# Two-layer hybrid decoder: value halves added after a trip through memory, query zeros kept, softmax reciprocals as a power on GpSimd

## The chip, the cores and the metric

The kernel runs on one core of a Trainium2 chip, as one launch for both layers. The metric is the device time of that launch in microseconds. The engines are named as the profile names them: PE (TensorE), PEld (its weight loads), DVE (VectorE), ACT (ScalarE), POOL (GpSimd), SP (SyncE, which issues the DMAs).

## What is computed

Two decoder layers over 1024 tokens of width 1024, all in fp32 accuracy. A layer projects x into four groups of heads with a token mixer each: gMLP (a), latent attention with a rotary part (b), dilated sliding-window attention (c) and a chunkwise mLSTM (d). The four results are concatenated, projected, added to the residual and normalised, and a SwiGLU feed-forward follows. Only b, c and the projection are touched here.

```python
def reference(x, positions, w_in, ...):
    for l in range(DEPTH):
        z = x @ w_in[l]
        z_a, z_b, z_c, z_d = jnp.split(z, [A_COLS, A_COLS + B_COLS, A_COLS + B_COLS + C_COLS], axis=-1)
        y_a = _gmlp_mixer(z_a, a_ln_g[l], a_ln_b[l], a_ws[l], a_bs[l])
        y_b = _mla_mixer(z_b, positions, b_q_norm[l], b_kv_norm[l], b_w_uq[l], b_w_ukv[l])
        y_c = _dilated_mixer(z_c, positions)
        y_d = _mlstm_mixer(z_d, d_conv_w[l], d_conv_b[l], d_igate_b[l], d_fgate_b[l])
        y = jnp.concatenate([y_a, y_b, y_c, y_d], axis=-1) @ w_out[l]
        x = _layer_norm(DEEPNORM_ALPHA * x + y, ln1_g[l], ln1_b[l])
        h = (jax.nn.silu(x @ w_gate[l]) * (x @ w_up[l])) @ w_down[l]
        x = _layer_norm(DEEPNORM_ALPHA * x + h, ln2_g[l], ln2_b[l])
    return x
```

## The kernel before, in words

PE multiplies fp32 numbers as a high and a low part (type fp32r), so most operands exist twice: ACT casts the high part, and DVE or POOL subtracts it from the source to get the low one (`split`, L145; for weights `prep_w`, L131 and L136). A tile framework puts the instructions of ACT, DVE, POOL and SP into an order; the order of PE in the attention is the one in which the code issues them (`manual_schedule` with `MAN`). Each engine runs its instructions strictly in order.

**Attention (`attn`).** A layer has four groups of two heads: G0 and G1 for the dilated mixer (mask `maskC`), G2 and G3 for the latent one (`maskB`, and a rotary part `R`, `QR`). A group is 16 rows, a row being one head with 128 queries; the 64 rows of a layer are numbered through, 0 to 63. Row by row `scores` multiplies queries and keys (tile `sc`), DVE adds the mask and takes the row minimum `mn` (L815), ACT takes the exponential and its sum `rs` (L819), DVE the reciprocal of the sum (L821), POOL multiplies the row `P` by it (L822). Three rows later `turn` transposes `P` on PE (`pt`, L839) and ACT and DVE split it into `PH` and `PL`; two rows later `values` multiplies with the values for each pair of rows (`pv`, L860). The value matrix holds its high part in columns 0 to 63 and its low part in 64 to 127, so `pv` comes out as two halves of 64 partitions that have to be added: ACT copies both into one tile `tmp` (L872, L873), POOL adds them (L874). For G0 and G1 a DMA writes the sum to `ys` in memory (L876), for G2 and G3 it stays in the tiles `Yb`. Four of the 32 pairs are `full`: their values are plain fp32 and only one half exists.

**Queries.** `put_q` fills two tiles for each head (q1, q2). q1 holds the high part of 64 rows twice, in both halves of the partitions (L786 and L788, ACT, from PSUM), q2 the low part in one half (L787) and zeros in the other (L789, POOL, a multiplication of the identity by 0). `qk_tiles` takes new tiles for each group.

**Jobs between rows.** Work for later groups is cut into jobs that `fill` spreads over the rows of the current one: in G0 the end of the projection `zc` and the queries and keys of G1; in G1, from `b_vqr_jobs`, the rotary queries of the latent groups (`rot`: PE `prb`, then rotation on DVE, L1026 to L1032, into `qr`), their values (`vals`: PE `pvb`) and the transposition of `qr` (`turn`: PE `ptr`, L1043, evacuated by L1046 and L1047). Both layers have the same program.

**Projection (`out_proj`).** The first four weight tiles `wO` are split during the last rows of the attention (L131 on ACT, L136 on POOL). `ysplit` loads the mixers' results from `ys` into tiles `yr` (pool "r", two buffers, shared with the raw weights) and splits them into `yT` (L145); g counts the quarter of the columns, and only g of 1 comes from `Yb`.

```python
        jobs = [start]
        for t2 in range(4):
            jobs += [f(rot, t2), f(vals, t2), f(turn, t2)]
        jobs += [f(rotk, half) for half in range(2)]
```

Of the kernel before, what the change touches and what calls it, by code (L numbers as in the profile page):

```python
# [13 lines left out]
L = 2  # L14
# [43 lines left out]
class Net:  # L58
# [89 lines left out]
    def consts(self):  # L148
        nc, cp, io = self.nc, self.cp, self.io
        self.ident = cp.tile([128, 128], F32, name="ident")  # L150
        nc.sync.dma_start(self.ident, io["c_ident"])
        self.identr = cp.tile([128, 128], F32R, name="identr")
        nc.vector.tensor_copy(self.identr, self.ident)
        sel = cp.tile([128, 8], F32, name="self32")
        nc.sync.dma_start(sel, io["c_sel"])
        self.sel = cp.tile([128, 8], F32R, name="sel")
        nc.vector.tensor_copy(self.sel, sel)
        self.mhalf = cp.tile([128, 8], F32, name="mhalf")
        nc.vector.memset(self.mhalf, -0.5)
        self.triu = cp.tile([128, 128], F32, name="triu")  # L160
# [621 lines left out]
    def put_q(self, pq, q1, q2, cols):  # L782
        nc = self.nc
        for hh in range(2):
# [3 lines left out]
            nc.scalar.copy(q1[hh][o, cols], pq[r, :])  # L788
            nc.gpsimd.tensor_scalar(out=q2[hh][o, cols], in0=self.ident[o, 0:1].to_broadcast([64, 512]), scalar1=0.0, scalar2=None, op0=ALU.mult)  # L789

    def attn(self, groups):
# [6 lines left out]
        def scores(n):  # L798
# [21 lines left out]
            def norm():  # L820
                nc.vector.reciprocal(rs[:, 1:2], rs[:, 0:1])  # L821
# [27 lines left out]
        def values(n):  # L849
# [25 lines left out]
            if spill is not None:  # L875
                nc.sync.dma_start(spill, y)  # L876
# [100 lines left out]
    def b_vqr_jobs(self, ct, w, out):  # L977
# [98 lines left out]
    def attention(self, l, zc, zjobs, ct):  # L1076
        nc, io = self.nc, self.io
        yv = lambda Y, g: [Y[0][:, g, :], Y[1][:, g, :]]
        bb = {}
        G = [dict(scale=sc, ahead=a, pp=p, full=f) for sc, a, p, f in zip((0.125, 0.125, 96 ** -0.5, 96 ** -0.5), AHEADS, PPS, FULL)]  # L1080
        for f in self.prep_c_jobs(zc[0], G[0]):
# [6 lines left out]
        def start0():  # L1088
            m = self.u("maskC")
            nc.sync.dma_start(m, io["c_maskC"])  # L1090
            G[0].update(mask=m, spill=(l, 0))
            self.jobs = zjobs + self.prep_c_jobs(zc[1], G[1])

        def start1():
            G[1].update(mask=G[0]["mask"], spill=(l, 1))
            w = box["w"] = self.b_weights(l)

            def st():
                bb["qk"] = self.qk_tiles("E", ("E", "B"))
            self.jobs = self.b_vqr_jobs(ct, w, bb) + [st] + self.b_qk_jobs(0, ct, w, bb, "qk")  # L1100

        def start2():
            m = self.u("maskB")
            nc.sync.dma_start(m, io["c_maskB"])
            box["Yb"] = [self.u("Yb", F32, "A").rearrange("p (a n) -> p a n", a=2) for _ in range(2)]
            bb["qk1"] = self.qk_tiles("A")
            G[2].update(mask=m, Y=yv(box["Yb"], 0), qk=bb["qk"], V=bb["V"][0], R=bb["R"], QR=bb["QR"][0])
            self.jobs = self.b_qk_jobs(1, ct, box["w"], bb, "qk1")

        def start3():  # L1110
            G[3].update(mask=G[2]["mask"], Y=yv(box["Yb"], 1), qk=bb["qk1"], V=bb["V"][1], R=bb["R"], QR=bb["QR"][1])
# [61 lines left out]
    def out_proj(self, l, Yb, xsrc):  # L1173
# [432 lines left out]
    def build(self):  # L1606
        self.open(B=8, w=10, r=2, E=10)
        T = [[None, None] for _ in range(KD)]
        for l in range(self.layers):
# [9 lines left out]
            self.dump(f"yb{l}", yb)  # L1619
# [5 lines left out]
def layouts(inp):  # L1625
# [42 lines left out]
    o["c_ident"] = np.eye(128, dtype=np.float32)  # L1668
    sel = np.zeros((128, 8), np.float32)
# [40 lines left out]
```

## Time and profile before

| what | value |
|---|---|
| median of 3 runs | 2476.17 us (2475.47 to 2478.26) |
| the profiled execution: time, span | 2477.19 us, 2475.5 us |
| PE busy | 2373.0 us (96%) |
| DVE, ACT, POOL busy | 67%, 42%, 53% |
| mean granted clock of PE | 0.983 |
| attention, layer 1 | about 260 to 460 us of the span |
| attention, layer 2 | about 1495 to 1695 us of the span |

Shares of the whole span say little here: most of the span is feed-forward, in which PE is busy without a gap. What the change can win or lose is read in the two stretches of attention and just behind them, where PE has gaps. The profile names for each gap the instruction whose end released it; "P L822" is the multiplication of a row by its reciprocal, "mn L815" its minimum, and so on.

### The profile page before, as it was taken

The page shows a single profiled execution, that of the slowest core. Times are in us where ns is not written, and L with a number is a line of the kernel's source. Part 1 is how long each engine was busy: PE and PEld are TensorE (multiplying, and loading weights), DVE is VectorE, ACT ScalarE, POOL GpSimd, SP SyncE. Part 2 cuts the span into 40 slices and gives each one's busy share as a digit, 9 for nine tenths or more (in the row PEclk, how much of TensorE's full clock was granted, in tenths as well). Part 3 has the DMA queues.
Part 4 walks back from the last instruction along what each step waited for, and adds up shares of the span by engine and source line. Part 5 has one row for each costly group of instructions (what it writes and reads, how often), then busy time and mean ns, then how long its engine had stood idle before and what let it go on. Part 6 is the DMA issues. An engine that isn't in the chain of part 4 may idle for free.

```text
span 2475.5 us, 33577 instructions
## 1 busy us (share of the span) xinstructions
PE 2373.0 (96%) x11820; PEld 1992.1 (80%) x11820; DVE 1662.9 (67%) x2978; ACT 1040.0 (42%) x2102; POOL 1308.8 (53%) x1172
## 2 busy tenths in 40 slices
PE   9999878998999999999999999789989999999997
PEld 9889867786888888788797898677868888887886
DVE  7743687478665664789957436873786655647999
ACT  6322669534323323543333226685343333235432
POOL 2124536667554554786622245366675554547865
PEclk9999999998999999999999999999989999999999
DMA  4111001421332322743221110014213323327431
GB/s 165 53 34 48 18 10 56 162 94 43 128 111 81 111 98 97 268 164 128 95 69 53 39 50 11 18 56 154 102 44 119 111 81 114 107 101 257 166 120 68
DMA packets 82198, 235.27 MB, mean 95 GB/s; under 512 B 10784, under 2 KB 13152, under 8 KB 82032
## 3 DMA queue, kind: packets, MB, share of 16 engines
q1 hardware_dynamic: 82032, 233.14, 27.3%
q8 instruction: 94, 1.54, 0.3%
q14 instruction: 72, 0.59, 0.1%
HBM read 172.78 MB, written 60.33 MB: 94 GB/s over the span
## 4 chain that ended last, share of the span: by engine, by line
PE 76%; DVE 11%; ACT 5%; POOL 4%; issue 3%; DMA 1%; POOLq 0%; DVEq 0%; ACTq 0%; SPq 0%
PE gu L123 33%; PE dn L123 13%; PE zc L123 5%; PE po L123 4%; PE zvo L568 4%; PE zdq L520 3%; PE za L123 3%; PE zb L123 2%; PE sc L123 2%; PE pv L860 2%; DVE P L815 1%; PE pt L839 1%; ACT P L819 1%; DVE PL L145 1%; POOL x L1132 1%
## 5 line engine op out<-in xcount | busy, mean ns | idle before, releaser
L123 PE MATMUL gu<-T,fc 128*128 128x512 f32 x2640 | 639.6, 399 | 17.0 <-POOL T L1340 5.9
L123 PEld LDWEIGHTS gu<-T,fc 128*128 128x128 f32 x2640 | 502.4, 191 | 140.6 <-POOL T L1340 8.8
L1265 POOL TENSOR_TENSOR fc<-fw,fc 128x512 fp32r<-128x512 f32 x264 | 374.2, 1421 | 362.4 <-ACT fc L1264 358.1
L123 PE MATMUL dn<-dc,dc 128*128 128x512 f32 x1512 | 354.8, 397 | 4.9 <-DVE dc L1265 4.9
L123 PEld LDWEIGHTS dn<-dc,dc 128*128 128x128 f32 x1512 | 286.2, 189 | 73.1 <-DVE dc L1265 5.7
L1264 ACT CAST fc<-fw 128x512 fp32r<-128x512 f32 x264 | 162.8, 621 | 409.2 <-PE gu L123 264.1
L123 PE MATMUL gu<-B,fc 128*128 128x512 f32 x1056 | 260.6, 395 | 0.0
L145 POOL TENSOR_TENSOR dc<-hr,dc 128x512 fp32r<-128x512 f32 x126 | 195.0, 1562 | 87.6 <-ACT dc L142 80.8
L123 PEld LDWEIGHTS gu<-B,fc 128*128 128x128 f32 x1056 | 197.8, 188 | 47.0
L1389 DVE TENSOR_TENSOR Ra<-Ra,gu 128x512 f32<-128x512 f32 x172 | 117.8, 686 | 162.7 <-PE gu L123 157.6
L822 POOL TENSOR_SCALAR P<-P,rs 128x256 f32<-128x256 f32 (+7 forms) x128 | 98.7, 775 | 125.7 <-DVE rs L821 100.3
L123 PE MATMUL po<-wh,yT 128*128 128x512 f32 x512 | 162.2, 396 | 0.0
L123 PE MATMUL zc<-wh,xT 128*128 128x384 f32 x512 | 134.0, 339 | 0.0
L136 POOL TENSOR_TENSOR wl<-raw,wh 128x768 fp32r<-128x768 f32 (+2 forms) x40 | 81.8, 2050 | 82.4 <-ACT wh L131 81.7
L123 PE MATMUL sc<-kst,q 128*128 128x512 f32 (+3 forms) x384 | 111.5, 387 | 12.5 <-DVE mn L815 12.5
L839 PE MATMUL pt<-ident,P 128*128 128x128 f32 x576 | 93.1, 287 | 23.5 <-DVE PL L145 15.0
L123 PEld LDWEIGHTS po<-wh,yT 128*128 128x128 f32 x512 | 95.7, 188 | 21.8
L1265 DVE TENSOR_TENSOR dc<-dr,dc 128x512 fp32r<-128x512 f32 x72 | 90.2, 1264 | 32.9 <-ACT dc L1264 32.8
L142 ACT CAST dc<-hr 128x512 fp32r<-128x512 f32 x126 | 77.7, 622 | 82.1 <-DMA hr<-hs 53.8
L819 ACT ACTIVATE P<-P,mn 128x256 f32<-128x256 f32 (+7 forms) x128 | 99.4, 778 | 29.1 <-DVE mn L815 28.3
L145 DVE TENSOR_TENSOR PL<-pt,PH 128x512 fp32r<-128x512 f32 (+3 forms) x176 | 95.1, 557 | 21.4 <-ACT PH L142 20.3
L123 PE MATMUL po<-wl,yT 128*128 128x512 f32 x256 | 100.2, 394 | 0.0
(377 smaller groups left out, 4999.9 us busy)
## 6 DMA issues: line engine op xcount, KB each, us to landing
fw<-in_wGU SPq DMA_DIRECT2D x88, 512.0 KB, 4.4
hr<-hs SPq DMA_DIRECT2D x142, 256.0 KB, 3.0
dr<-in_wD SPq DMA_DIRECT2D x44, 512.0 KB, 6.2
hs<-Ra SPq DMA_DIRECT2D x40, 512.0 KB, 2.9
hs<-Rb SPq DMA_DIRECT2D x22, 512.0 KB, 5.4
raw<-in_wO SPq DMA_DIRECT2D x16, 512.0 KB, 3.5
x<-x SPq DMA_DIRECT2D x16, 512.0 KB, 2.6
raw<-in_wC SPq DMA_DIRECT2D x16, 384.0 KB, 3.0
```

The source lines that it names most:

```text
L123: self.nc.tensor.matmul(out, lhsT=a, rhs=b, start=first and j == 0, stop=last and j == n - 1)
L136: (eng or nc.gpsimd).tensor_sub(lo[:, :n], raw[:, :n], f32(hi[:, :n]))
L142: nc.scalar.copy(hi, src)
L145: (lo_eng or nc.vector).tensor_sub(lo, src, f32(hi))
L520: step(lambda: nc.tensor.matmul(pz, lhsT=a, rhs=b_, start=n == 0, stop=n == 23))
L568: nc.tensor.matmul(box["p"], lhsT=a, rhs=b_, start=j == 0, stop=j == 23)
L819: nc.scalar.activation(P[:, 0:nk], P[:, 0:nk], AF.Exp, scale=-1.0, bias=m, accum_out=rs[:, 0:1])
L822: nc.gpsimd.tensor_scalar(out=P[:, 0:nk], in0=P[:, 0:nk], scalar1=rs[:, 1:2], scalar2=1.0, op0=ALU.mult, op1=ALU.mult)
L839: nc.tensor.transpose(pt[:, b * 128:(b + 1) * 128], P[:, (b0 + b) * 128:(b0 + b + 1) * 128], self.ident)
L1264: nc.scalar.copy(dst[:, 0:512], src)
L1265: lo_eng.tensor_sub(dst[:, 512:1024], src, f32(dst[:, 0:512]))
L1389: tt = lambda o, a, b, op: v.tensor_tensor(out=o, in0=a, in1=b, op=op)
```

## The change

1. **Reciprocal.** `rs` to the power of -1 on POOL (new line L828, with a tile `minus` of -1) in place of DVE's reciprocal L821. The multiplication behind it is now L829.
2. **Queries.** The second copy of the high part is a POOL copy from the first copy in SBUF (L796) in place of ACT's cast from PSUM. The zero halves are written once a tile, at its full width of 1024 columns (L780, the mask times 0), and the tiles q2 of G0 and G1 are used again by G2 and G3. `maskC` is loaded earlier.
3. **Values.** For G0, G1 and G2 ACT copies both halves of `pv` at once (128 partitions), and two DMAs write them apart to a new array `yp` (for full pairs the second DMA writes zeros). For G3 ACT copies one half and DVE adds the other half from PSUM into the one tile `Yb`.
4. **Projection.** `ysplit` loads pairs of halves from `yp` (three loads for each h, in place of one) and DVE adds them.
5. **Jobs.** `turn` of a pair of blocks comes one `rot` later; one pair of `QR` tiles moves to other pools.

Per layer that takes from DVE 64 reciprocals and gives it 8 additions of 64x256 (G3) and 6 of 128x512 (`yp`); takes from ACT 16 casts of 64x512 and turns 56 copies of 64x256 into 20 of 128x256 and 8 of 64x256; takes from POOL 16 multiplications of 64x512 and 28 additions of 64x256 and gives it 64 powers of 128x1, 16 copies of 64x512 and 4 multiplications of 64x1024. SP issues 48 writes of halves where it issued 16 of sums, and 10 loads for `ysplit` where it issued 6.

```diff
@@ qk_tiles, put_q
+    def qk_tiles(self, pool, q2=None):
+        f = lambda n: self.u(n, F32R, pool)
+        kst, q1 = [f("kst") for _ in range(2)], [f("q1") for _ in range(2)]
+        if q2 is None:
+            q2 = [f("q2") for _ in range(2)]
+            for hh in range(2):
+                o = slice(64 - 64 * hh, 128 - 64 * hh)
+                self.nc.gpsimd.tensor_scalar(out=q2[hh][o, :], in0=self.mask[o, :], scalar1=0.0, scalar2=None, op0=ALU.mult)
+        return kst, q1, q2
...
-            nc.scalar.copy(q1[hh][o, cols], pq[r, :])
-            nc.gpsimd.tensor_scalar(out=q2[hh][o, cols], in0=self.ident[o, 0:1].to_broadcast([64, 512]), scalar1=0.0, scalar2=None, op0=ALU.mult)
+            nc.gpsimd.tensor_copy(q1[hh][o, cols], f32(q1[hh][r, cols]))
@@ scores
-                nc.vector.reciprocal(rs[:, 1:2], rs[:, 0:1])
+                nc.gpsimd.tensor_tensor(out=rs[:, 1:2], in0=rs[:, 0:1], in1=self.minus, op=ALU.pow)
@@ values
+            tmp = self.t2("tmp", 256)
             if "Y" in G:
+                y = G["Y"][64 * hh:64 * hh + 64, jp * 256:(jp + 1) * 256]
+                if full:
+                    nc.scalar.copy(y, pv[0:64, 0:256])
+                else:
+                    nc.scalar.copy(tmp[0:64, :], pv[0:64, 0:256])
+                    nc.vector.tensor_tensor(out=y, in0=tmp[0:64, :], in1=pv[64:128, 0:256], op=ALU.add)
+                return
+            nc.scalar.copy(tmp[0:m, :], pv[0:m, 0:256])
+            for part in range(2):
+                dst = G["spill"][part][64 * hh:64 * hh + 64, jp * 256:(jp + 1) * 256]
+                nc.sync.dma_start(dst, self.io["c_zero"][:, 0:256] if full and part else tmp[64 * part:64 * part + 64, :])
...
-                nc.scalar.copy(tmp[0:64, 0:256], pv[0:64, 0:256])
-                nc.scalar.copy(tmp[0:64, 256:512], pv[64:128, 0:256])
-                nc.gpsimd.tensor_tensor(out=y, in0=tmp[0:64, 0:256], in1=tmp[0:64, 256:512], op=ALU.add)
@@ b_vqr_jobs
-        for t2 in range(4):
-            jobs += [f(rot, t2), f(vals, t2), f(turn, t2)]
-        jobs += [f(rotk, half) for half in range(2)]
+        jobs += [f(rot, 0), f(vals, 0)]
+        for t2 in range(1, 4):
+            jobs += [f(rot, t2), f(turn, t2 - 1), f(vals, t2)]
+        jobs += [f(rotk, 0), f(turn, 3), f(rotk, 1)]
@@ out_proj, ysplit
-                if g != 1:
+                if g in (0, 3):
...
+                    y = [Yb[:, h * 512:h * 512 + 512]] * 2
+                    for f in range(2 if g == 2 else 1):
+                        raw = self.uw("yr", F32, "r")
+                        nc.sync.dma_start(raw[:, 0:1024].rearrange("p (a n) -> p a n", a=2),
+                                          io["yp"][l, f if g == 2 else 2][:, :, h * 512:h * 512 + 512].rearrange("a p n -> p a n"))
+                        y[f] = raw[:, 0:512]
+                        nc.vector.tensor_tensor(out=y[f], in0=y[f], in1=raw[:, 512:1024], op=ALU.add)
```

**Three places where instructions move.** The names carry the numbers of their buffers; `P` and `rs` of one row stand in one line with each other.

First place: PE in G1 of the first layer, from the first `vals` (`pvb`) on. Before:

```order
L123 MATMUL pvb_3408<-wk_3321,kvT_2202 128x256
L839 MATMUL pt_3423<-ident,P_3259 128x128 x4
L123 MATMUL sc_3431<-kst_2936,q_448_2938 128x256
L123 MATMUL sc_3431<-kst_2936,q_450_2940 128x256
L1043 MATMUL ptr_3439<-ident,qr_3404 128x128
L1043 MATMUL ptr_3439<-ident,qr_3406 128x128
...
L839 MATMUL pt_3453<-ident,P_3281 128x128 x4
L839 MATMUL pt_3460<-ident,P_3281 128x128 x2
...
L123 MATMUL prb_3479<-wq_3313,cqT_2203 128x128
```

The same place in the changed kernel:

```order
L123 MATMUL pvb_3406<-wk_3320,kvT_2204 128x256
L846 MATMUL pt_3421<-ident,P_3257 128x128 x4
L123 MATMUL sc_3429<-kst_2936,q_448_2938 128x256
L123 MATMUL sc_3429<-kst_2936,q_450_2940 128x256
L123 MATMUL prb_3437<-wq_3312,cqT_2205 128x128
...
L846 MATMUL pt_3456<-ident,P_3279 128x128 x4
L846 MATMUL pt_3463<-ident,P_3279 128x128 x2
...
L1048 MATMUL ptr_3482<-ident,qr_3402 128x128
L1048 MATMUL ptr_3482<-ident,qr_3404 128x128
```

The transposition `ptr` of the first `qr` has moved behind the second `prb`, another row's transposition `pt` and another row's scores.

Second place: POOL in G2 and G3 of the first layer, rows 47 to 51 (`P` of 768, 128, 896, 256 and 1024 columns) with the four weight splits (`wl`, L136). Before:

```order
L822 TENSOR_SCALAR P_4596<-P_4596,rs_4608 128x768
L822 TENSOR_SCALAR P_4633<-P_4633,rs_4640 128x128
L136 TENSOR_TENSOR wl_5241<-raw_5238,wh_5240 128x1024
L874 TENSOR_TENSOR Yb_4075<-tmp_4657 64x256
L136 TENSOR_TENSOR wl_5247<-raw_5244,wh_5246 128x1024
L822 TENSOR_SCALAR P_4676<-P_4676,rs_4688 128x896
L822 TENSOR_SCALAR P_4699<-P_4699,rs_4706 128x256
L136 TENSOR_TENSOR wl_5253<-raw_5250,wh_5252 128x1024
L874 TENSOR_TENSOR Yb_4074<-tmp_4747 64x256
L822 TENSOR_SCALAR P_4722<-P_4722,rs_4734 128x1024
```

The same rows in the changed kernel, from the multiplication of the row of 128 columns on:

```order
L829 TENSOR_SCALAR P_4610<-P_4610,rs_4617 128x128
L136 TENSOR_TENSOR wl_5210<-raw_5207,wh_5209 128x1024
L136 TENSOR_TENSOR wl_5216<-raw_5213,wh_5215 128x1024
L828 TENSOR_TENSOR rs_4665<-rs_4665,minus 128x1
L828 TENSOR_TENSOR rs_4683<-rs_4683,minus 128x1
L829 TENSOR_SCALAR P_4653<-P_4653,rs_4665 128x896
L829 TENSOR_SCALAR P_4676<-P_4676,rs_4683 128x256
L136 TENSOR_TENSOR wl_5222<-raw_5219,wh_5221 128x1024
L828 TENSOR_TENSOR rs_4711<-rs_4711,minus 128x1
L828 TENSOR_TENSOR rs_4741<-rs_4741,minus 128x1
L136 TENSOR_TENSOR wl_5228<-raw_5225,wh_5227 128x1024
L829 TENSOR_SCALAR P_4699<-P_4699,rs_4711 128x1024
```

The additions `Yb` are gone; the powers of two rows stand together ahead of the two multiplications; and the fourth weight split stands ahead of the multiplication of row 51, where it stood behind it.

Third place: POOL at the start of G0 in the first layer, rows 0 to 3. Before:

```order
L822 TENSOR_SCALAR P_2842<-P_2842,rs_2848 128x128
L822 TENSOR_SCALAR P_2859<-P_2859,rs_2869 128x896
L822 TENSOR_SCALAR P_2879<-P_2879,rs_2885 128x256
L756 TENSOR_TENSOR zcq_2555<-ra_2916 128x128
L757 TENSOR_TENSOR zck_2556<-ra_2916 128x128
L822 TENSOR_SCALAR P_2895<-P_2895,rs_2905 128x1024
```

In the changed kernel:

```order
L828 TENSOR_TENSOR rs_2869<-rs_2869,minus 128x1
L828 TENSOR_TENSOR rs_2885<-rs_2885,minus 128x1
L758 TENSOR_TENSOR zcq_2557<-ra_2916 128x128
L759 TENSOR_TENSOR zck_2558<-ra_2916 128x128
L828 TENSOR_TENSOR rs_2905<-rs_2905,minus 128x1
L829 TENSOR_SCALAR P_2842<-P_2842,rs_2848 128x128
L829 TENSOR_SCALAR P_2859<-P_2859,rs_2869 128x896
```

All four powers now stand ahead of the first multiplication, so row 0 is multiplied only after the sum of row 3 is there.

## Rows read from the trace of the kernel before

**Rows 1.** Busy time by window, layer 1: window, length; engines; granted clock, DMA share, GB/s.

```profile
280.00:460.00 180.00, 149.87 (x976) 128.52 (x975) 141.42 (x411) 145.04 (x346) 99.89 (x109) 0.95 0.11 33
300.00:360.00 60.00, 46.49 (x311) 39.46 (x311) 49.76 (x143) 38.40 (x100) 18.22 (x22) 0.94 0.04 10
420.00:440.00 20.00, 17.14 (x107) 14.69 (x104) 13.09 (x40) 17.50 (x43) 19.56 (x19) 0.91 0.42 132
460.00:480.00 20.00, 20.00 (x93) 16.41 (x92) 5.56 (x7) 7.45 (x16) 12.06 (x10) 1.00 0.87 315
```

**Rows 2.** PE's waits from 255 to 460: releaser, us in total, times, longest.

```profile
PE pt L839 <- DVE PL L145: 7.0, 10, 1.4
PE ptr L1043 <- DVE qr L1032: 7.0, 5, 3.3
PE sc L123 <- DVE mn L815: 6.5, 9, 2.1
PE pv L860 <- ACT q L788: 2.4, 1, 2.4
```

**Rows 3.** Line L821, both layers: durations; DVE's idle time before it; who waited for it.

```profile
L821 DVE RECIPROCAL rs<-rs x128: 144/162/167, 275.0 to 1690.4; 128x1 f32<-128x1 f32 x128
  ACT P L819: 17.3, 44
  POOL P L822: 100.3, 53
```

**Rows 4.** POOL's groups by shape, 255 to 460: busy us, mean ns; idle before.

```profile
L789 POOL TENSOR_SCALAR q<-ident 64x512 fp32r<-64x512 f32 x16 | 23.7, 1487 | 1.4 <-PE zc L123 0.7
L874 POOL TENSOR_TENSOR Yb<-tmp 64x256 f32<-64x256 f32 x14 | 10.2, 727 | 6.9 <-ACT tmp L873 2.7 <-DVE rs L821 2.5 <-PE sc L123 1.3
L874 POOL TENSOR_TENSOR tmp<-tmp 64x256 f32<-64x256 f32 x12 | 9.2, 771 | 8.2 <-ACT tmp L873 7.2 <-POOL P L822 0.8
L822 POOL TENSOR_SCALAR P<-P,rs 128x1024 f32<-128x1024 f32 x8 | 9.0, 1121 | 9.4 <-DVE rs L821 8.4 <-ACT V L142 0.9
L822 POOL TENSOR_SCALAR P<-P,rs 128x512 f32<-128x512 f32 x8 | 5.5, 691 | 3.9 <-DVE rs L821 3.1 <-PE pt L839 0.6
```

**Rows 5.** Another power of this shape on POOL, whole span: by shape; then min/median/max ns.

```profile
L287 POOL TENSOR_TENSOR rs<-rs,mhalf 128x1 f32<-128x1 f32 x48 | 36.1, 751 | 3.8
L287 POOL TENSOR_TENSOR rs<-rs,mhalf x48: 547/804/988, 33.4 to 2469.2; 128x1 f32<-128x1 f32 x48
```

**Rows 6.** ACT's and DVE's groups by shape, 255 to 460.

```profile
L872 ACT COPY tmp<-pv 64x256 f32<-64x256 f32 x27 | 9.8, 363 | 4.8 <-PE pv L860 2.9 <-issue 1.7
L788 ACT CAST q<-ptc 64x512 fp32r<-64x512 f32 x8 | 4.6, 581 | 1.0 <-DVE q L787 0.7
L1026 DVE TENSOR_TENSOR ra<-prb,cs 128x256 f32<-128x256 f32 x4 | 1.7, 417 | 0.1
L1032 DVE TENSOR_TENSOR qr<-ra 128x512 f32<-128x512 f32 x8 | 5.8, 761 | 0.1
```

**Rows 7.** Timelines of DVE and PE in G1: start us, us, instruction, idle before and releaser.

```profile
326.43 0.16 DVE L821 RECIPROCAL rs<-rs 128x1 f32<-128x1 f32 x1 [0.97 <-ACT P L819]
328.49 2.27 PE L1043 MATMUL ptr<-ident,qr 128*128 128x128 f32 x8 [3.29 <-DVE qr L1032]
```

**Rows 8.** Timelines of POOL and PE around row 51.

```profile
417.84 2.44 POOL L136 TENSOR_TENSOR wl<-raw,wh 128x1024 fp32r<-128x1024 f32 x1
...
428.22 1.47 POOL L822 TENSOR_SCALAR P<-P,rs 128x1024 f32<-128x1024 f32 x2
...
429.39 0.66 PE L839 MATMUL pt<-ident,P 128*128 128x128 f32 x4 [0.61 <-POOL P L822]
```

**Rows 9.** Timelines of PE and ACT near rows 0 to 3.

```profile
279.25 0.27 PE L839 MATMUL pt<-ident,P 128*128 128x128 f32 x1
...
280.66 0.19 ACT L819 ACTIVATION_READ_ACCUMULATOR P<-P,mn 128x1 f32 x1
...
283.31 0.41 PE L839 MATMUL pt<-ident,P 128*128 128x128 f32 x2 [1.58 <-POOL P L822]
```

More of the change, by code (lines that the diff above doesn't have):

```diff
@@ L159, in consts @@
         nc.vector.memset(self.mhalf, -0.5)
+        self.minus = cp.tile([128, 1], F32, name="minus")
+        nc.vector.memset(self.minus, -1.0)
         self.triu = cp.tile([128, 128], F32, name="triu")
@@ L995, in start @@
                          for i in range(3)] for f in FULL[2:]]
-            out["QR"] = [[self.u("QR", F32R, "A").rearrange("p (h n) -> p h n", h=2) for _ in range(2)] for _ in range(2)]
+            out["QR"] = [[self.u("QR", F32R, p).rearrange("p (h n) -> p h n", h=2) for p in two] for two in ("EB", "AA")]
         def vals(t2):
@@ L1077, in attention @@
         nc, io = self.nc, self.io
-        yv = lambda Y, g: [Y[0][:, g, :], Y[1][:, g, :]]
         bb = {}
         G = [dict(scale=sc, ahead=a, pp=p, full=f) for sc, a, p, f in zip((0.125, 0.125, 96 ** -0.5, 96 ** -0.5), AHEADS, PPS, FULL)]
+        self.mask = self.u("maskC")
+        nc.sync.dma_start(self.mask, io["c_maskC"])
         for f in self.prep_c_jobs(zc[0], G[0]):
@@ L1088, in start0 @@
         def start0():
-            m = self.u("maskC")
-            nc.sync.dma_start(m, io["c_maskC"])
-            G[0].update(mask=m, spill=(l, 0))
+            G[0].update(mask=self.mask, spill=io["yp"][l, 0])
             self.jobs = zjobs + self.prep_c_jobs(zc[1], G[1])
         def start1():
-            G[1].update(mask=G[0]["mask"], spill=(l, 1))
+            G[1].update(mask=G[0]["mask"], spill=io["yp"][l, 1])
             w = box["w"] = self.b_weights(l)
             def st():
-                bb["qk"] = self.qk_tiles("E", ("E", "B"))
+                bb["qk"] = self.qk_tiles("E", G[0]["qk"][2])
             self.jobs = self.b_vqr_jobs(ct, w, bb) + [st] + self.b_qk_jobs(0, ct, w, bb, "qk")
@@ L1104, in start2 @@
             nc.sync.dma_start(m, io["c_maskB"])
-            box["Yb"] = [self.u("Yb", F32, "A").rearrange("p (a n) -> p a n", a=2) for _ in range(2)]
-            bb["qk1"] = self.qk_tiles("A")
-            G[2].update(mask=m, Y=yv(box["Yb"], 0), qk=bb["qk"], V=bb["V"][0], R=bb["R"], QR=bb["QR"][0])
+            box["Yb"] = self.u("Yb", F32, "A")
+            bb["qk1"] = self.qk_tiles("A", G[1]["qk"][2])
+            G[2].update(mask=m, spill=io["yp"][l, 2], qk=bb["qk"], V=bb["V"][0], R=bb["R"], QR=bb["QR"][0])
             self.jobs = self.b_qk_jobs(1, ct, box["w"], bb, "qk1")
         def start3():
-            G[3].update(mask=G[2]["mask"], Y=yv(box["Yb"], 1), qk=bb["qk1"], V=bb["V"][1], R=bb["R"], QR=bb["QR"][1])
+            G[3].update(mask=G[2]["mask"], Y=box["Yb"], qk=bb["qk1"], V=bb["V"][1], R=bb["R"], QR=bb["QR"][1])
         for g, f in zip(G, (start0, start1, start2, start3)):
@@ L1183, in ysplit @@
             for g in range(4):
-                y = Yb[h]
-                if g != 1:
+                if g in (0, 3):
                     raw = self.uw("yr", F32, "r")
-                    nc.sync.dma_start(raw[:, 0:1024], io["ys"][l, (0, 0, 2, 1)[g], h])
-                    y = raw[:, 0:1024].rearrange("p (a n) -> p a n", a=2)
+                    nc.sync.dma_start(raw[:, 0:1024], io["ys"][l, g // 3, h])
+                    y = [raw[:, 0:512], raw[:, 512:1024]]
+                else:
+                    y = [Yb[:, h * 512:h * 512 + 512]] * 2
[5 more added lines that the diff above has]
+                        nc.vector.tensor_tensor(out=y[f], in0=y[f], in1=raw[:, 512:1024], op=ALU.add)
                 for f in range(2):
@@ L1191, in ysplit @@
                     t = self.u("yT", F32R, "y" if g == 1 and h == 1 else "A").rearrange("p (a n) -> p a n", a=2)
-                    self.split(t[:, 0, :], t[:, 1, :], y[:, f, :], lo_eng=nc.vector if g == 1 else nc.gpsimd)
+                    self.split(t[:, 0, :], t[:, 1, :], y[f], lo_eng=nc.vector if g == 1 else nc.gpsimd)
                     TY[k][h] = t
@@ L1668, in layouts @@
     o["c_ident"] = np.eye(128, dtype=np.float32)
+    o["c_zero"] = np.zeros((64, 1024), np.float32)
     sel = np.zeros((128, 8), np.float32)
```

18 lines of the change are left out of this document (2 added, 16 removed).

## The prediction

> **What bounds the kernel now.** I read the busy time by window first, then PE's list of waits, then the lines that change, then timelines at the places where the order moves. The windows [rows 1] say where there is anything to win. From 460 us on PE is busy without a gap (20.00 of 20.00), and the feed-forward behind it, most of the span, is untouched. In the attention of layer 1, from 280 to 460, PE is busy 149.87 of 180 us. So the gaps are 180 - 149.87 = 30.1 us in a layer, and the second layer, whose program is the same, is taken as equal. Twice 30.1, 60 us, is the most the change could give back. DVE is at 49.76 of 60 us from 300 to 360, ACT at 145.04 of 180 over all of it, POOL at 99.89, except from 420 to 440, where POOL is at 19.56 of 20: there POOL is the full engine.
>
> PE's waits [rows 2] name who ends the gaps: DVE with the low part `PL` (7.0 us), DVE with the rotated queries `qr` (7.0 us in five waits, one of 3.3), DVE with the minima `mn` (6.5 us), and one wait of 2.4 us behind ACT's second query cast. So the engine whose work the change lightens most is the one that PE waits for, but the work goes to POOL, and POOL runs its instructions in order.
>
> **The change, term by term, for one layer.**
>
> Reciprocal off DVE. Half of the 128 reciprocals of 162 ns [rows 3] is 64 x 0.16 = 10.2 us of DVE's time. Worse than their length is that DVE stood idle before them until ACT's sum came: 17.3 us in 44 cases, 8.7 a layer [rows 3]. One is seen at 326.43, after 0.97 us idle [rows 7]; the rotation that PE then waits 3.29 us for stands behind it. Added to DVE are 8 additions of 64x256 from PSUM at about 0.42 (128x256, the L1026 row) [rows 6] = 3.3. Net, DVE is relieved of 10.2 + 8.7 - 3.3 = 15.6 us, a tenth of its time. ACT loses 16 casts of 0.58 = 9.3, and 28 pairs of copies of 0.363 become 28 single ones, so another 10.2: 19.5 us [rows 6]. The waits this can shorten are those for `PL` and `mn`, 13.5 us. A chain that ends on DVE is partly PE's own work and ACT's, so I take back less than a third: **-4.0** (bounds 0, when something else is late at once, and -8).
>
> Turn one rot later. The `ptr` waits are 7.0 us [rows 2]. In the new order one `prb`, a row's transposition and a row's scores stand between `qr` and its `ptr`; that is work PE has anyway, and it covers more than the longest wait of 3.3. But a gap that is closed early lets the next late result show. I take two thirds: **-4.5** (0 to -7.0).
>
> Second query copy off ACT. It ends the 2.4 us wait before `pv` [rows 2], as ACT no longer holds the exponential behind it. **-2.0** (0 to -2.4).
>
> POOL's sum. Gone are 16 zeroings of 1.487 (23.7) and the additions (10.2 + 9.2 = 19.4) [rows 4]. The powers: the nearest row is a power of the very shape 128x1 by another constant tile, 751 ns in the mean, 547 to 988 [rows 5]; I take the mean, and 64 of them are 48 us. The Trainium skill (GPSIMD Engine Reference, Engine selection) speaks against such a move: elementwise work with two inputs belongs on VectorE, as GpSimd is about two times slower. By that factor a power would be an estimated 0.32 us (2 x 0.16), 20 us in all. The row is nearly five times the reciprocal's 0.16, and the row decides. The 16 copies of 64x512 lie between 0.69 (L822 of 512 columns, one input read in a row) and 1.49 (L789, a broadcast input) [rows 4]; I take 0.69, since the input is read in a row too: 11.0. The 4 zeroings of 64x1024 at 1.12 (L822 of 1024 columns) are 4.5. POOL's change: 48 + 11.0 + 4.5 - 23.7 - 19.4 = +20 us a layer, on 99.89 of 180. There is room on the whole, and a row's power mostly replaces a wait of its multiplication (100.3 us in 53 cases, both layers [rows 3]). It is paid where POOL is full or its order is bad, at two places.
>
> Row 51. Before, the first weight split begins at 417.84 and the multiplication of row 51 starts at 428.22; PE already waits 0.61 us for it [rows 8]. In the new order, two additions of 0.73 leave this stretch, the powers of rows 47 to 52, six of 0.75, come in, and the fourth weight split, 2.42 us long by its like at 417.84, passes ahead of the multiplication. 4.5 + 2.4 - 1.5 = 5.4 us later, less some small gaps of POOL. PE has no slack there. What PE does while it waits also takes over waits it had in this window, 20 - 17.14 = 2.9 us [rows 1]. **+4.0** (+2.0 when the powers are 0.55 and all of the 2.9 goes, +6.5 when they are near 1.0).
>
> Start of G0. Row 0's multiplication now waits for the power of row 3, whose sum comes at 280.85 [rows 9]; with 0.75 for that power, row 0's transposition starts at 281.6 at the earliest and not at 279.25. Of these 2.4 us up to 1.58, the wait of PE at 283.31 [rows 9], may be taken over. **+1.5** (0 to +2.4).
>
> Values and projection. The spills leave through DMA queues that are nearly empty here (DMA share 0.11) [rows 1]. In `out_proj` DVE gets 6 additions of 128x512 at 0.76 (the L1032 row [rows 6]), 4.6 us, in a stretch where it is busy 5.56 of 20 [rows 1], but five loads in place of three pass the same two buffers, and the split of one quarter comes about when PE needs it: **+0.5** (0 to +3). Keeping the zeros, the pools of `QR` and the earlier mask load count nothing: their cover is POOL's spare time before row 0.
>
> Sum: -4.0 - 4.5 - 2.0 + 4.0 + 1.5 + 0.5 = -4.5 us a layer, -9.0 for both. The profiled execution took 2477.19 us; it lies 1.0 above the median of 2476.17, so I forecast 2477.2 - 9.0 - 1.0 = **2467 us** against that median.
>
> **The rivals.** About 0.2% (5 us; below 2471.2, above 2481.1) is what a measurement of this kernel can tell from no change.
>
> 1. *POOL's order decides, and it is slower.* One mechanism: rows wait in POOL's queue behind powers of other rows whose sums aren't there yet, and behind weight splits. It decides once a power takes about 1.0 us and a copy 1.49, so that POOL has no spare time around rows 33 to 36 (where the copies stand between multiplications), row 51 and row 0. Then the losses are +6.5 + 2.4 + 3 (four copies, each 0.8 longer) = 11.9, the projection's 0.5 comes on top, and of the 10.5 gained some 8.5 are left: +3.9 a layer, 2476.2 + 7.8 = 2484 us. For it: POOL at 19.56 of 20 in one window, PE without slack at row 51. Against it: 80 us of POOL's 180 are free.
>
> 2. *The freed time is hidden anyway.* DVE and ACT are early, but PE waits for a chain of sum, power, multiplication that is as long as before, and the moved `ptr` exposes the next wait. Gains of 6 meet losses of 5.5: about 2475 us. For it: 64 rows each still go PE, DVE, ACT, POOL, PE. Against it: most of the listed waits end on DVE.
>
> 3. *More goes.* DVE is what holds the attention from 280 to 420, and with a tenth of its work and its idle waits gone the whole row pitch shortens; the two places on POOL cost half of what I take. Gains of 7 + 7.0 + 2.4, losses of 3.5: -13 a layer, about 2450 us.
>
> 4. *The power is cheap.* If POOL took it in twice the reciprocal's 0.16 us [rows 3], 0.32, row 51 would lose 6 x 0.43 = 2.6 less and the start 0.4 less: -7.5 a layer, 2461 us. The 751 ns row [rows 5] leaves little for it. This is the time by the rule of the Trainium skill's page named above. That the change doesn't do what it says I don't count: the order rows show it on the engines.
>
> **How the numbers follow.** Forecast, 2457 to 2474 by the terms' middle bounds: 0.44 (with rival 4's 0.04, 0.48). Rival 3: 0.13. Rival 2: 0.18. Rival 1: 0.21. Faster by over 0.2% are rival 3 and nearly all of the forecast and rival 4: 0.58. Slower by over 0.2%: rival 1, less its lower edge: 0.19. Within: 0.23. The range leaves out most of rival 3 and the upper third of rival 1: 2453 to 2486.
>
> **What would show it.** In the profile of the changed kernel: no DVE reciprocal and no DVE idle time that ends on ACT's sum; `ptr` waits below 2 us a layer; no wait of 2.4 us before `pv`; DVE busy about 7 us less a layer and ACT some 19 less; powers near 0.75 us; PE waiting some 4 to 5 us for the multiplication of row 51, and 2 to 3 us near row 0; PE's gaps from 280 to 460 near 25 us. The prediction is wrong if `ptr` or `PL` waits stay as they are, if the powers are over 1 us, or if PE starts to wait for `yT` behind the attention.

## The result: slower, and the profile after

The changed kernel takes 2490.35 us (median of 4 runs, 2486.52 to 2495.36) against 2475.82 us before: a ratio of 1.0062 (95% interval 1.0048 to 1.0076), so about 15 us slower. The forecast was 9 us faster, with 2486 as the upper end of the range; it was wrong in sign. The profiled execution below took 2486.52 us, the fastest of the four, with a span of 2484.7 us; it lies 9 us above the one before, less than the medians do.

Busy time by window of the changed kernel, layer 1, in the columns of [rows 1]:

```profile
280.00:460.00 180.00, 149.01 (x967) 128.24 (x966) 136.11 (x360) 126.01 (x305) 108.19 (x153) 0.93 0.16 46
300.00:360.00 60.00, 48.75 (x331) 41.14 (x329) 48.82 (x129) 39.54 (x104) 26.43 (x38) 0.94 0.08 17
420.00:440.00 20.00, 15.28 (x91) 13.73 (x90) 10.30 (x29) 11.72 (x27) 15.06 (x17) 0.83 0.40 119
```

ACT is 19 us lighter, as forecast, and DVE 5 us. PE's gaps did not shrink: 31.0 us where there were 30.1. POOL has grown by 8 us, not 20, but two zeroings of 5.6 us together stand just ahead of this window, so its work grew by about 13.5 us a layer (35.8 + 9.7 + 11.1 new, below, and 23.7 + 19.4 gone [rows 4]). The longest of PE's waits, 255 to 520, say where the gaps went (compare [rows 2]):

```profile
PE pt L846 <- POOL P L829: 9.5, 4, 4.7
PE pt L846 <- DVE PL L145: 4.6, 5, 2.0
PE sc L123 <- DVE mn L822: 4.6, 9, 1.1
PE pv L867 <- DVE ra L1033: 2.6, 1, 2.6
PE ptr L1048 <- DVE R L997: 2.5, 1, 2.5
PE ptc L922 <- DVE kst L788: 1.5, 1, 1.5
```

In the kernel before, the wait for POOL's multiplication stood further down the same list:

```profile
PE pt L839 <- POOL P L822: 2.2, 2, 1.6
```

The waits on `qr` and behind ACT's second query cast are gone and those on `PL` and `mn` are shorter, but two new ones on DVE's `ra` and `R` have come in, and PE now waits 9.5 us for POOL's multiplication, in four waits. POOL's new instructions, by shape, from 255 to 470:

```profile
L828 POOL TENSOR_TENSOR rs<-rs,minus 128x1 f32<-128x1 f32 x64 | 35.8, 564 | 61.6 <-ACT P L826 48.6 <-DVE PL L145 11.3 <-DVE mn L822 1.1
L780 POOL TENSOR_SCALAR q<-maskC 64x1024 fp32r<-64x1024 f32 x4 | 11.1, 2773 | 0.9 <-PE zc L123 0.7
L796 POOL CAST q<-q 64x512 fp32r<-64x512 f32 x16 | 9.7, 608 | 7.7 <-ACT q L794 7.3
L829 POOL TENSOR_SCALAR P<-P,rs 128x1024 f32<-128x1024 f32 x8 | 9.0, 1125 | 0.4
```

Powers and copies are cheaper than forecast (0.564 and 0.608 us for 0.75 and 0.69). A zeroing is two and a half times dearer: 2.77 us, not 1.12. Where it hurts stands in the timelines of POOL and PE at the start of G0:

```profile
274.88 5.62 POOL L780 TENSOR_SCALAR q<-maskC 64x1024 fp32r<-64x1024 f32 x2 [0.68 <-PE zc L123]
280.47 0.57 POOL L828 TENSOR_TENSOR rs<-rs,minus 128x1 f32<-128x1 f32 x1
...
283.70 0.54 POOL L828 TENSOR_TENSOR rs<-rs,minus 128x1 f32<-128x1 f32 x1
284.35 2.92 POOL L829 TENSOR_SCALAR P<-P,rs 128x128 f32<-128x128 f32 x4
...
284.77 0.48 PE L846 MATMUL pt<-ident,P 128*128 128x128 f32 x1 [4.70 <-POOL P L829]
```

The two zeroings for G1 hold POOL for 5.6 us; then the four powers pass. PE transposes row 0 at 284.77, where it did so at 279.25 [rows 9]. Row 51, at 426 to 431:

```profile
426.43 1.08 POOL L828 TENSOR_TENSOR rs<-rs,minus 128x1 f32<-128x1 f32 x2
427.46 2.38 POOL L136 TENSOR_TENSOR wl<-raw,wh 128x1024 fp32r<-128x1024 f32 x1
429.79 1.49 POOL L829 TENSOR_SCALAR P<-P,rs 128x1024 f32<-128x1024 f32 x2
...
430.99 1.97 PE L846 MATMUL pt<-ident,P 128*128 128x128 f32 x8 [4.10 <-POOL P L829]
```

That is the wait that was forecast, about in its size and by its cause: the fourth weight split ahead of the multiplication. It was 0.61 us before [rows 8].

To see where the time goes I compare, row by row, when PE begins a row's transposition in a trace and in that of before, and take by how much the difference grows over a stretch. The stretches run from the layer's first `zc` product to row 5, on to rows 36, 50 and 63, and from there to the 61st product of the feed-forward. Mean of the two layers, in us (negative is won):

| run | to row 5 | 5 to 36 | 36 to 50 | 50 to 63 | behind |
|---|---|---|---|---|---|
| the change | 7.1 | -12.0 | 1.4 | 4.7 | 4.7 |
| zero_dve | 0.7 | -11.6 | 2.0 | 4.4 | 4.7 |
| no_power | 4.2 | -8.9 | -0.8 | -1.4 | 6.1 |
| zero_dve_no_power | 0.7 | -8.6 | -0.8 | -1.5 | 6.2 |
| old_turn | 5.7 | -11.0 | 0.8 | 4.0 | 5.5 |
| queries_turn | 0.4 | -8.4 | 0.0 | -0.6 | 0.7 |
| queries | 0.8 | -8.0 | 0.0 | -1.3 | 0.6 |
| queries_values | 0.8 | -11.5 | -0.7 | -1.5 | 6.2 |
| keep_zeros | 1.5 | -2.4 | 0.6 | -0.7 | 0.1 |
| copy_only | -0.3 | 1.5 | 2.8 | -1.0 | 0.3 |
| power_c | 0.7 | -5.7 | -0.1 | -1.3 | 0.7 |
| queries_pool | 3.5 | -7.9 | 0.8 | -0.9 | 0.3 |
| values | -0.3 | -2.2 | -1.0 | -1.6 | 7.1 |
| power | 2.0 | -0.8 | 2.2 | 3.0 | -0.2 |

Each line is from one trace. In rows 5 to 36 its two layers differ by up to 3.3 us in most runs, by 4.3 in values (0.0 and -4.3) and by 5.3 in power (-3.4 and 1.9), so a difference of 2 or 3 us in this stretch is not firm. The change wins 12 us there, more than the 10.5 hoped for in all, and gives more back at the start, around row 51 and in the projection.

### The profile page after: what moved, and what is told of

Its sections match the earlier page's. It is cut to its first block, busy times and chain, and to the rows that moved or that the text cites. A ratio compares the mean times of both kernels' runs of the same rounds, so it can differ in the third digit from the quotient of the medians.

```text
span 2484.7 us, 33583 instructions
## 1 busy us (share of the span) xinstructions
PE 2366.7 (95%) x11820; PEld 1985.5 (80%) x11820; DVE 1662.7 (67%) x2879; ACT 998.0 (40%) x2014; POOL 1332.0 (54%) x1252
## 4 chain that ended last, share of the span: by engine, by line
PE 74%; DVE 11%; POOL 6%; issue 4%; ACT 3%; DMA 1%; POOLq 0%; DVEq 0%; ACTq 0%; SPq 0%
PE gu L123 33%; PE dn L123 13%; PE zc L123 5%; PE zvo L570 4%; PE zdq L522 3%; PE po L123 3%; PE za L123 3%; PE zb L123 2%; PE pv L867 2%; PE sc L123 2%; DVE P L822 1%; PE pt L846 1%; POOL x L1137 1%; DVE ma L1501 1%; POOL rs L289 1%
## 5 line engine op out<-in xcount | busy, mean ns | idle before, releaser
L828 POOL TENSOR_TENSOR rs<-rs,minus 128x1 f32<-128x1 f32 x128 | 71.9, 565 | 123.8 <-ACT P L826 104.7
L136 POOL TENSOR_TENSOR wl<-raw,wh 128x768 fp32r<-128x768 f32 (+2 forms) x40 | 81.7, 2048 | 85.2 <-ACT wh L131 84.8
L123 PE MATMUL sc<-kst,q 128*128 128x512 f32 (+3 forms) x384 | 113.4, 391 | 11.9 <-DVE mn L822 11.1
L846 PEld LDWEIGHTS pt<-ident,P 128*128 128x128 f32 x576 | 66.8, 146 | 48.3 <-POOL P L829 26.4
```

The source lines that it names most:

```text
L123: self.nc.tensor.matmul(out, lhsT=a, rhs=b, start=first and j == 0, stop=last and j == n - 1)
L136: (eng or nc.gpsimd).tensor_sub(lo[:, :n], raw[:, :n], f32(hi[:, :n]))
L828: nc.gpsimd.tensor_tensor(out=rs[:, 1:2], in0=rs[:, 0:1], in1=self.minus, op=ALU.pow)
L846: nc.tensor.transpose(pt[:, b * 128:(b + 1) * 128], P[:, (b0 + b) * 128:(b0 + b + 1) * 128], self.ident)
```

## Experiments

All medians are of kernels run beside the kernel before; ratios are to it.

| run | median us | ratio, 95% interval |
|---|---|---|
| zero_dve | 2475.89 | 0.9997, 0.9987 to 1.0007 |
| no_power | 2469.29 | 0.9969, 0.9956 to 0.9982 |
| zero_dve_no_power | 2464.82 | 0.9946, 0.9932 to 0.9961 |
| old_turn | 2485.77 | 1.0035, 1.0024 to 1.0046 |
| queries_turn | 2458.18 | 0.9926, 0.9909 to 0.9942 |
| queries | 2459.13 | 0.9925, 0.9910 to 0.9939 |
| queries_values | 2463.90 | 0.9947, 0.9931 to 0.9962 |
| values | 2480.60 | 1.0024, 1.0011 to 1.0036 |
| keep_zeros | 2476.10 | 1.0006, 0.9994 to 1.0017 |
| copy_only | 2480.82 | 1.0016, 1.0003 to 1.0028 |
| power_c | 2465.72 | 0.9959, 0.9946 to 0.9972 |
| dve_sums | 2457.51 | 0.9924, 0.9903 to 0.9945 |
| values_w1 | 2491.49 | 1.0063, 1.0048 to 1.0078 |
| power | 2494.41 | 1.0070, 1.0054 to 1.0086 |
| queries_pool | 2467.74 | 0.9962, 0.9948 to 0.9976 |

**Two places on GpSimd (zero_dve, no_power, both).**

```diff
-self.nc.gpsimd.tensor_scalar(out=q2[hh][o, :], in0=self.mask[o, :], scalar1=0.0, ...
+self.nc.vector.tensor_scalar(out=q2[hh][o, :], in0=self.mask[o, :], scalar1=0.0, ...
...
-nc.gpsimd.tensor_tensor(out=rs[:, 1:2], in0=rs[:, 0:1], in1=self.minus, op=ALU.pow)
+nc.vector.reciprocal(rs[:, 1:2], rs[:, 0:1])
```

> The four zeroings a layer move from GpSimd to VectorE; all else is the changed kernel. Theory (two queue places on GpSimd cost the time): GpSimd spends 2.77 us on each zeroing, and the two for G1 stand ahead of row 0's power, so PE waits 4.7 us for row 0 and row 5 is 8.4 us late in layer 1. Without them row 0 of layer 1 is no more than 1.5 us later than in the kernel before, and the total falls by 2 x 4 to 2 x 7 us, to about 2476 to 2483 us. Rival (the late start is caught up anyway in rows 15 to 36, where the changed kernel gains 10 us): the total falls by less than 3 us. The 4 us wait at row 51 stays by both.

> The reciprocal goes back to VectorE; all else is the changed kernel. Theory: the wait at row 51 (4.1 us, 4.8 in the other layer) falls below 1.5 us, the start keeps its 5.6 us of zeroings ahead of row 0 but loses the four powers, so row 0 is 3 to 4.5 us late and not 5.5; the total falls by 2 x 4 to 2 x 6 us, to 2478 to 2482 us. Rival (taking the reciprocal off VectorE is what won the 10 us in rows 15 to 36): these rows win 5 us or less in a layer, and the total stays within 3 us of the changed kernel.

> Both edits: zeroings and reciprocals on VectorE. Theory: start and row 51 are both as in the kernel before, the gain of the moved turn and of the copies off ScalarE is left, less 1.7 us a layer in the projection: 2466 to 2472 us. Rival (the reciprocal's move won rows 15 to 36): 2475 to 2480 us.

Off GpSimd, the zeroings give back 16 us (1.0062 to 0.9997), a little over the 8 to 14 that were expected; row 5 is 0.7 us late where it was 7.1. Without them the framework also puts row 0's multiplication right behind its power, ahead of the other rows' powers, so this run undoes both faults of the start, and the 16 us are not the zeroings' alone. With no power in the kernel they cost 6 us (no_power against zero_dve_no_power) or 9 (queries_pool against queries, below). Without the power 23 us are gone (1.0062 to 0.9969), more than expected, of which 6 a layer are at rows 50 to 63; the rival is half right, as rows 5 to 36 win 3 us a layer less. Both edits give 2464.82, 1 us below the expected span. PE's waits for POOL, in zero_dve (255 to 470):

```profile
PE pt L846 <- POOL P L829: 5.3, 4, 4.1
```

and in no_power:

```profile
PE pt L846 <- POOL P L829: 2.3, 2, 1.8
```

The first keeps row 51's wait of 4.1 us. The second has it no more: there the fourth weight split stands behind the multiplication of row 51 again.

**The order of turn (old_turn, queries_turn, queries, queries_values).** old_turn is the changed kernel with the old list of jobs; the other three are built up from the kernel before, all with the query part and its zeros on VectorE.

```diff
-jobs += [f(rot, t2), f(turn, t2 - 1), f(vals, t2)]
+jobs += [f(rot, t2), f(vals, t2), f(turn, t2)]
```

> The old order of the jobs (turn right behind its own rot and vals); all else is the changed kernel. Theory: the waits of PE for the rotated queries are back, 5 to 7 us a layer, and the total rises by 6 to 12 us to 2496 to 2502 us. Rival (the lighter VectorE alone takes these waits away): within 3 us of the changed kernel.

> The kernel before with two parts of the change alone: the query part (copies on GpSimd, zeros kept, but written by VectorE) and the new order of turn. Values, projection and reciprocals are as before. Against the run zero_dve_no_power (2464.8 us) it lacks the value part alone. Theory (the value halves give little in the attention and cost 4 to 5 us a layer behind it, as the first projections and the first products of the feed-forward come later): the rows up to 63 are within 2 us a layer of that run, the 4 to 5 us behind are gone, 2455 to 2459 us. Rival (ACT's 10 us and GpSimd's 19 us that the value part saves made the gain of rows 5 to 36): rows 5 to 36 win 4 us a layer or less where that run wins 8.7, and the total is 2465 us or more.

> The query part alone on the kernel before, zeros written by VectorE. Theory (the moved turn is worth nothing, as its wait only changes its name): within 3 us of queries_turn. Rival (the prediction's term for turn, 4.5 us a layer): 7 to 10 us slower than queries_turn.

> Query part (zeros on VectorE) and value part on the kernel before; old order of turn, reciprocals on VectorE. Theory: within 3 us of the run zero_dve_no_power, 2462 to 2468 us. Rival (turn is worth its term): 2472 us or more.

The new order is worth nothing: queries_turn against queries is 0.9926 to 0.9925, zero_dve_no_power against queries_values 0.9946 to 0.9947, and in the full change the old order is even some 5 us faster, so that old_turn failed both its expectations; the other three came in the expected spans. The wait changes its name. In queries (old order), 255 to 470:

```profile
PE ptr L1048 <- DVE qr L1037: 5.0, 6, 2.0
```

In queries_turn (new order) these are gone, and there stand instead

```profile
PE ptr L1048 <- DVE R L997: 3.4, 1, 3.4
PE pv L865 <- DVE ra L1033: 2.7, 1, 2.7
```

`rotk` now precedes the last `turn`, and its DVE work delays it; the rotation of the next blocks delays a `pv`. These runs also show what made the 12 us of the middle: the query part alone wins 8 of them, and with the value part, in the old order and without the power, 11.5 (queries_values). Beside the value part the new order wins 3 less (zero_dve_no_power), though the totals are the same.

**What wins in the query part (keep_zeros, copy_only, queries_pool).** keep_zeros puts ACT's second cast back into queries, copy_only makes only the copy on GpSimd, queries_pool leaves the zeroings on GpSimd. keep_zeros also has the other pools and the earlier mask load that go with the kept zeros.

```diff
-nc.gpsimd.tensor_copy(q1[hh][o, cols], f32(q1[hh][r, cols]))
+nc.scalar.copy(q1[hh][o, cols], pq[r, :])
```

> One half of the query part on the kernel before: zero halves written once (by VectorE) and kept, so that GpSimd loses its 16 zeroings of 1.49 us a layer; the second query copy stays on ScalarE, from PSUM. The run queries, with both halves, won 8 us a layer in rows 5 to 36. Theory (the zeroings stood between the multiplications: in the kernel before, rows 6, 27, 28 and 33 waited 3.4 to 5.5 us on GpSimd behind them): this half makes 4 to 6 of the 8 us, total 2463 to 2468 us. Rival (ScalarE is what is short, and the copy taken off it won the time): 2 us a layer or less, 2471 us or more.

> The other half: the second query copy on GpSimd, in place of ScalarE's cast from PSUM; GpSimd's 16 zeroings of 1.49 us stay. Theory: 2 to 3 us a layer won in rows 5 to 36 (the one wait of 2.4 us of the prediction), given back in part by 16 more copies of 0.6 us in GpSimd's queue, total 2471 to 2476 us. Rival: 5 us a layer or more, 2464 to 2467 us.

> The query part alone as the change has it: the four zeroings a layer on GpSimd, ahead of row 0; all else as in the kernel before. Against the run queries (2459 us, zeros on VectorE). Theory (5.6 us of GpSimd ahead of row 0, but no powers): row 5 of layer 1 is 3 to 4 us later than before, where queries has 1.6; total 2462 to 2466 us. Rival (the loss of the zeroings needs the powers): within 2 us of queries.

Neither half wins by itself (1.0006, 1.0016), together they are at 0.9925. Both expectations failed in the total. In the kernel before, POOL's timeline shows what the zeroings did:

```profile
361.50 6.05 POOL L789 TENSOR_SCALAR q<-ident 64x512 fp32r<-64x512 f32 x4
367.65 1.47 POOL L822 TENSOR_SCALAR P<-P,rs 128x768 f32<-128x768 f32 x2
```

The sums of these two rows had their reciprocals at 362.33 and 364.25 us, so the first waited 5.3 us on POOL behind four zeroings. Without these keep_zeros wins 4.9 us a layer from row 5 to row 27, and then loses half of it again, by row 36, in a wait of 3.5 us that the second cast on ACT leaves (`pv` behind `kst`):

```profile
PE pv L865 <- DVE kst L786: 3.5, 1, 3.5
```

copy_only puts 16 copies into POOL's queue with the zeroings still there and wins nothing. The gain is that of a pair: POOL must be freed for the copies, and ACT of them. queries_pool gives 9 us of it back, 2.7 a layer at the start, and ends 1.7 us above its expected span: the zeroings cost time ahead of row 0 with no power near. On VectorE they are also shorter, 0.78 us each for 2.77 on GpSimd; in zero_dve:

```profile
L780 DVE TENSOR_SCALAR q<-maskC x8: 691/778/839, 257.2 to 1510.9; 64x1024 fp32r<-64x1024 f32 x8
```

No run parts the place from the length.

**The power alone (power, power_c).** power is the first part of the change by itself; power_c is queries_turn with the power in G0 and G1 alone.

```diff
-nc.vector.reciprocal(rs[:, 1:2], rs[:, 0:1])
+(nc.gpsimd.tensor_tensor(out=rs[:, 1:2], in0=rs[:, 0:1], in1=self.minus, op=ALU.pow) if R is None else
+ nc.vector.reciprocal(rs[:, 1:2], rs[:, 0:1]))
```

> The power alone on the kernel before, sums and zeroings of GpSimd as before. Theory (the power costs the rows in GpSimd's queue): slower, by 3 to 8 us a layer, with 3 us or more of them between rows 50 and 53: 2482 to 2492 us. Rival (the prediction's term, 4 us won a layer, half of it lost at row 51): 2470 to 2476 us.

> On the run queries_turn (2458.2 us) the reciprocals of G0 and G1 alone become powers on GpSimd; G2 and G3, where the weight splits stand in GpSimd's queue, keep VectorE's reciprocal. Theory (the power loses by its place in the queue, not by its own 0.55 us): rows 5 to 36 win 2 to 4 us a layer more, nothing is lost at row 51, total 2450 to 2455 us. Rival (a power on GpSimd costs a row as much as it saves): 2456 us or more.

Alone it costs 17 us, where 6 to 16 were expected. PE's waits for POOL in power, 255 to 470:

```profile
PE pt L841 <- POOL P L824: 11.9, 7, 5.9
```

In power_c it loses too (0.9926 to 0.9959), though no power is near the weight splits and nothing is lost at row 51 (-1.3), so my theory that only the place at row 51 makes it lose fell. Its loss lies in rows 5 to 36, and PE waits only 1.3 us there for POOL's multiplication, so why it loses stays open: a row's chain from the sum to the multiplication is also some 0.4 us longer with a power than with a reciprocal, and no run parts that from the place in the queue. Against zero_dve_no_power the powers of zero_dve win 3 us a layer in rows 5 to 36. But queries_values, in the old order of turn, has the same -11.5 without a power, so the 3 us may be only what the new order had lost. In no pair of runs does the power win in the total.

**The value part (values, values_w1, dve_sums).** values is the value part alone on the kernel before; values_w1 moves the second weights ahead of the second `ysplit`; dve_sums is queries_turn with G2's and G3's sums on DVE, without any trip through memory.

```diff
+W1 = [self.prep_w(io["wO"][l, 1, j], 1024, p="v") for j in range(4)]
 ysplit(1)
 proj(1, 0, W0)
-W1 = [self.prep_w(io["wO"][l, 1, j], 1024, p="v") for j in range(4)]
...
-nc.scalar.copy(tmp[0:64, 256:512], pv[64:128, 0:256])
-nc.gpsimd.tensor_tensor(out=y, in0=tmp[0:64, 0:256], in1=tmp[0:64, 256:512], op=ALU.add)
+nc.vector.tensor_tensor(out=y, in0=tmp[0:64, 0:256], in1=pv[64:128, 0:256], op=ALU.add)
```

> The value part alone on the kernel before. Theory (little won in the attention, 4 to 5 us a layer lost behind it): 2480 to 2486 us. Rival (the value part made the gain of rows 5 to 36): 2460 to 2470 us.

> The run values, with the second set of projection weights loaded and split ahead of the second half's value loads (two lines of out_proj change places). Theory (the value part's loss behind the attention is the second weights' loads, which SP issues behind the longer chain of value loads: at 490 us in values and 494.6 us in the changed kernel, at 479.7 before): the loads are issued before 482 us, the projection's last blocks end one after the other again, and of the 4.2 us a layer that values loses between the first projection and the first products of the feed-forward at least 3 are gone; total 2472 to 2476 us. Rival (the loss is the second half's own values, which come late): the loss stays or grows, 2480 us or more.

> On the run queries_turn the sums of the value halves of G2 and G3 are made by VectorE from PSUM (as the change does for G3), in place of a second ScalarE copy and an addition on GpSimd; G0 and G1 and the projection are as before. Theory (the value part's gain of 2.5 to 3 us at rows 50 to 63 comes from the additions that leave GpSimd's queue there, its loss from the trip through memory): 2 to 3 us a layer won at rows 50 to 63, no loss in the projection, total 2452 to 2455 us. Rival (VectorE is short there too): within 2 us of queries_turn.

The value part loses 6 us in all, and 7 a layer behind the attention. SP's queue shows what may be a part of why. Second weights in the kernel before:

```profile
479.67 10.40 SPq L128 DMA_DIRECT2D raw<-in_wO  x4
```

and in the changed kernel:

```profile
494.57 10.53 SPq L128 DMA_DIRECT2D raw<-in_wO  x4
```

They share two buffers with ten value loads, where there were six. Their products end later, the normalisation starts later, and PE waits for it before the feed-forward (`ptx` on POOL's `x`, three waits, 2.3 us). values_w1 issues the second weights from 460 to 482 us, and those waits fall from 3.2 us in values to 0.4. But now the values are late, and the kernel is slower still (2491.49 us, where 2472 to 2476 were expected):

```profile
PE po L123 <- ACT yT L142: 8.4, 1, 8.4
```

So the cure was wrong. Whether the late weights are the cause isn't shown either, as PE reaches those waits 8.4 us later here and the weights have that much more time. The two traces fit the reading that whichever goes last through the two buffers is late; more buffers weren't tried. What is shown is that the loss behind the attention comes with the value part (6.2 in queries_values, 0.6 in queries). dve_sums is level with queries_turn (2457.51 and 2458.18), as its rival had it, so the 2 to 3 us that were expected of it can't be told from none.

## Why the prediction was wrong, point by point

Summed over both layers, and measured by the run that has the part alone:

| part | forecast, us | measured, us |
|---|---|---|
| power: reciprocal off DVE, row 51, start of G0 | +3.0 | +17.3 (power) |
| order of turn | -9.0 | 0 (queries_turn against queries) |
| second query copy, kept zeros | -4.0 | -9.4 (queries_pool) |
| values and projection | +1.0 | +5.9 (values) |
| sum | -9.0 | +13.9 |

The parts nearly add: the change itself measured +15.3. The step that failed most is the power. The prediction let it cost something at two places only, as "a row's power mostly replaces a wait of its multiplication"; in the run power, PE waits 11.9 us in layer 1 for POOL's multiplication where it waited 2.2. The gain counted for turn is the next. Term by term, for one layer:

- *Reciprocal off DVE, -4.0.* Not shown as a gain. Rows 5 to 36 win 3.0 by it in zero_dve against zero_dve_no_power, 0.8 in power, and queries_values wins as much there without it. Between the first two runs rows 36 to 50 lose 2.8 and rows 50 to 63 5.9, and 1.5 come back behind. By the ratios the power costs 12.6 us between these two runs, and 23 between the change and no_power.
- *Row 51, +4.0.* Right in place and cause: a wait of 4.1 us, 4.7 us lost from row 50 to 63. In size it is partly luck: with the measured 0.56 us for a power in place of 0.75 the prediction's own sum is 4.3 and not 5.4, before it takes off its discounts.
- *Start of G0, +1.5.* Near the mark for the power alone (2.0 in power). In the change 7.1 us were lost to row 5; with the zeroings but no power it is 4.2 (no_power), the block of four powers behind them adds the other 2.9, and without the zeroings the powers cost nothing there (0.7 in zero_dve and in zero_dve_no_power).
- *Zeroings, counted at nothing.* Wrong in price and in place, 6 to 16 us in all, by what else stands in the queue. The price was taken from a row with another kind of output (L822, f32), although L789 wrote fp32r by the very operation, at 1.487 for 512 columns: twice that is 2.97 for 1024, and 2.77 was measured. And there was no spare time before row 0: POOL's timeline has both zeroings directly ahead of row 0's power.
- *Turn, -4.5.* Zero. I reasoned from the longest wait, and not from what the moved job is put behind: DVE's work for `rotk` and the next rotation took its place.
- *Second query copy, -2.0.* By itself it wins nothing (copy_only). With the zeroings that leave POOL's queue the query part wins 8 a layer in rows 5 to 36. The sum of POOL's busy time, in which I had booked the zeroings, could not show that a row waited 5.3 us behind them.
- *Values and projection, +0.5.* Between 4.7 and 7.1 are lost behind the attention, of which a part is won on the way there (values: -2.2, -1.0, -1.6).

None of the prediction's three signs of being wrong came: the `ptr` waits fell from 7.0 to 3.0 us and the `PL` waits from 7.0 to 4.6, the powers took 0.56 us, and PE did not wait for `yT`. They watched the engines' prices and the old waits, and not the new wait for POOL's multiplication.

The mechanism nearest to what was measured is that of rival 1, POOL's order, with a chance of 0.21; but its condition, a power of about 1.0 us, wasn't needed, and its 2484 us fell short.

The power measured 564 ns to the reciprocal's 162 [rows 3]. The rule of the Trainium skill (GPSIMD Engine Reference, Engine selection) that two-input elementwise work belongs on VectorE points the right way here, and the cost was larger than its factor of two, though a power and a reciprocal are not the same operation. The same table has work with one input at roughly line rate on GpSimd; the zeroing, 2773 ns for 1024 columns on GpSimd beside 778 on VectorE, does not agree with it. L829, a multiplication with one tensor as input too, took 1125 for as many columns.

## What to carry to other kernels

An engine that is half idle is not free: what counts for an in-order queue is which instruction stands ahead of the one that the critical engine waits for, so read the generated order at the places without slack, and price every instruction in it. Take the price from the row with the same operation and output type. A wait that is closed by moving a job is gained only if the job that takes its place in the queue isn't late itself. The best kernels here, queries, queries_turn and dve_sums, can't be told apart: they take the query part with its zeros on VectorE and neither the power nor the trip through memory, at 0.9925 of the time before.

## What was not expected of the hardware

GpSimd's multiplication by zero into fp32r takes 2.77 us for 64x1024, while a copy into fp32r takes 0.608 for 64x512 and a multiplication into f32 1.125 for 128x1024; so neither the width nor the type alone explains it, and no run here parts these from the form of the instruction (one operation, where L829 has two). Between 420 and 440 us the granted clock is 0.83 where it was 0.91, behind the wait of 4.1 us: the lower of the two levels (1.2 GHz) lasts 6.8 us where it lasted 3.4. That the wait costs more than its length by this isn't shown, as zero_dve has the same wait with 0.91 from 415 to 435, and over the whole span the clock is 0.985 with the change and 0.983 before.
